# Fewer visits of TensorE to transposes, scores and values, and y's parts in the norm's tiles

## The chip, the core and the metric

The kernel runs on one core of one Trainium2 chip. The metric is the device time of one execution in microseconds (us). TensorE is the matmul engine (PE in the profile, PEld its weight loads), VectorE is DVE, ScalarE is ACT, GpSimd is POOL and SyncE is SP. Each engine works through its own queue of instructions in the order in which the program issues them, and waits on semaphores for the others.

## What is computed

The reference is one layer on 256 tokens of width 1024. Cut to what matters here:

```python
h = _rmsnorm(x, norm_w) * (1 + scale) + shift
(qa, ka, va, za, qm, km, vm, zm, om, ig, fg, ga, gm) = split(h @ w_in)
qa, ka = _rmsnorm(heads(qa, 8)), _rmsnorm(heads(ka, 8))
ya = (attention(qa, ka, va, rel_bias) * silu(za)) @ w_att_proj      # causal, 8 heads of 128
qm, km = split(silu(causal_conv(concat(qm, km))))
hm = mlstm(qm, km, vm, ig, fg)                                      # 4 heads of 256
ym = (rmsnorm(sigmoid(om) * hm) * silu(zm)) @ w_ml_proj
y = sigmoid(ga) * ya + sigmoid(gm) * ym
return x + gate * (y @ w_out)
```

All is float32. The large products are made of three fp32r matmuls: each operand is split into a high part and a low rest (names that end in h and l), and high x high, high x low and low x high are added up in PSUM.

## The kernel before

The first part, up to about 52 us, makes the norm (tiles hTh and hTl, h transposed, high and low part) and the first columns of h @ w_in. The rest, with which the change deals, is a list of 25 chunks of 512 output columns: the rest of ka, then two halves each of va, za, qm, km, att (the product with w_att_proj), zm, vm, om, ga, gm, ml (with w_ml_proj) and out (with w_out). A chunk has four steps, one for each pair of 128-row blocks of the weights, so that there are 100 steps: va is steps 4 to 11, za 12 to 19, qm 20 to 27, km 28 to 35, att 36 to 43, zm 44 to 51, vm 52 to 59, om 60 to 67, ga 68 to 75, gm 76 to 83, ml 84 to 91, out 92 to 99. A step is either 12 matmuls with 512 moving columns (kind "tok", lines L932 to L934, the activations are the stationary operand: va, zm, vm, om, out) or 24 matmuls with 256 moving columns (kind "ws", L939 to L942, the weights are the stationary operand: the others). For each step ScalarE casts the weights' high part (L424) and VectorE, for a few steps GpSimd, subtracts it (L428), four steps ahead of TensorE, into a ring of five buffers (wh, wl).

Between the matmuls of one step and the next, small work is put in by hand: at(step, function) calls the function just ahead of the step's matmuls, in the order in which the calls were registered, and between(step, function) calls it a little earlier, between the cast and the subtraction for the step four later. TensorE's share of this work are plain fp32 matmuls and transposes. One such stay of TensorE away from the weights' stream is called a visit here. The functions that matter:

- qk_T(which, half) transposes four heads of q or k: eight transposes (L468), four into each of two PSUM tiles named aux, and ScalarE copies each tile out (L470) to qT or kT.
- att_qk(h) (L577, L578): the scores of head h into an aux tile, which VectorE reads (L581, L583). att_exp(h): ScalarE's exponentials (L589, L590). att_norm(h): VectorE divides by the sums. att_PT(h): three transposes of the probabilities (L602 to L604).
- att_av(h0): probabilities times values for two heads (L615, L617). ml_scores(h): L716, L719. ml_T(kp): four transposes (L773) of mLSTM's result.
- gates_1, gates_2: small work on the gates. ScalarE's L512 in gates_2 waits for GpSimd's L505 in gates_1.
- ev_ml: makes y out of the last sums, with a cast to its high part and a subtraction for the low part (L705 to L708).

The aux tiles rotate over four PSUM banks in the order in which the program makes them: an aux tile can be written when the tile four before it has been read. mm tiles, the sums of a chunk, have two further places. SBUF is a set of named slots (s0 to s6, "bias"); a slot holds tiles that live one after the other, and FREE puts unused columns ahead of a slot, so that it sets where the tiles after it lie.

Of the kernel before, what the change touches and what calls it, by code (L numbers as in the profile page):

```python
# [10 lines left out]
F32R = mybir.dt.float32r  # L11
# [5 lines left out]
S = 256  # L17
KT = 8
# [46 lines left out]
def tile_hybrid(ctx: ExitStack, tc: tile.TileContext, x, c, params, params2, rel_t, w_row, ada_mod, ada_gate,  # L65
# [23 lines left out]
    hTh = consts.tile([128, KT, S], F32R, name="hTh")  # L89
    hTl = consts.tile([128, KT, S], F32R, name="hTl")  # L90
# [189 lines left out]
    for step in P1_STEPS:  # L280
        op, k = step[0], int(step[1])
# [42 lines left out]
    def done(name, half):  # L324
        return 4 * (C[name, half] + 1)
# [68 lines left out]
    SL = {}  # L394


    FREE = {'s2': 112, 's1': 80}

    def free(tag):
        if tag in FREE:  # L400
            hl.tile([128, FREE.pop(tag)], F32, name="free_" + tag, bufs=1)

    def slot(tag, shape, dt, name):
        free(tag)
        return hl.tile(shape, dt, name=name, tag=tag, bufs=1)
# [27 lines left out]
    def at(step, fn, *a):  # L433
        hooks.setdefault(step, []).append((fn, a))

    def between(step, fn, *a):
        hooks_between.setdefault(step, []).append((fn, a))

    T = {}
# [256 lines left out]

    def ev_ml(pt, half):
        if half == 0:
            for nm, tag, at0 in (("yh", "s2", 16), ("yl", "s6", 48)):
                t = slot(tag, [128, at0 + KT * S], F32R, nm)  # L700
                T[nm] = t[:, at0:].rearrange("p (k s) -> p k s", k=KT)
        for q in range(2):
            ks = slice(4 * half + 2 * q, 4 * half + 2 * q + 2)
            yf = hl.tile([128, 2, 256], F32, name="yf", tag="scr", bufs=2)
            nc.vector.tensor_tensor(yf, pt[:, 2 * q:2 * q + 2], T["gm"][:, ks], op=OP.mult)  # L705
            nc.vector.tensor_tensor(yf, yf, T["ga"][:, ks], op=OP.add)
            nc.scalar.copy(T["yh"][:, ks], yf)
            nc.vector.tensor_tensor(T["yl"][:, ks], yf, T["yh"][:, ks].bitcast(F32), op=OP.subtract)  # L708
# [97 lines left out]
    def ev_out(pt, c0, n, t):  # L806
# [5 lines left out]

    EV = dict(va=ev_va, za=ev_za, att=ev_att,
              zm=ev_zm, vm=ev_vm, om=ev_om, ga=ev_ga, gm=ev_gm, ml=ev_ml)

    at(0, q_scale)
# [7 lines left out]
    at(3, qk_norm, "q", 1)  # L824
    at(0, bias_read)
    at(4, gates_0)
    at(6, qk_T, "q", 0)
    at(7, qk_T, "k", 0)
    at(8, qk_T, "q", 1)
    at(7, qk_norm, "k", 1)  # L830
    at(10, qk_T, "k", 1)
    for h in range(AH):
        between(10 + h, att_norm, h)
        between(9 + h, att_qk, h)
        at(11 + h, att_PT, h)
        at(9 + h, att_exp, h)
    for step, fn in ((5, gates_1), (8, gates_2), (10, gates_3), (12, gates_copy), (13, gates_4), (15, gates_5),
                     (17, gates_6), (17, gates_T), (18, gates_7), (21, gates_D)):
        at(step, fn)
    for nm in ("qm", "km"):  # L840
        for hf in range(2):
            s = done(nm, hf)
# [2 lines left out]
                at(s + q + 1, conv_silu, hf, nm, q)  # L845
    for q in range(2):
        at(done("za", 0) + 1 + q, att_av, 2 * q)
        at(done("za", 1) + 1 + q, att_av, 4 + 2 * q)
    s = done("km", 0)
    at(s + 3, ml_scores, 0)  # L850
    at(s + 4, ml_scores, 1)
    s = done("km", 1)
    at(s + 3, ml_scores, 2)
    at(s + 4, ml_scores, 3)
    at(4 * C["att", 0] - 10, gate_init)
    gate_left = {}
    for q, nm in enumerate(GSEG):
        s = 4 * C[nm, 0] - 4
# [5 lines left out]
    for hp in range(2):  # L864
        s = done("om", hp)
        at(s + 1, ml_num, 2 * hp)
        at(s + 2, ml_num, 2 * hp + 1)
        at(s + 3, ml_y, hp)
        at(s + 7, ml_T, 2 * hp)
        at(s + 8, ml_T, 2 * hp + 1)  # L870

    A = HB - 1
# [21 lines left out]
    for g in range(NG):  # L894
# [30 lines left out]
        for kk in range(2):  # L925
            k = 2 * kp + kk
# [74 lines left out]
```

## Time and profile before

| | |
|---|---|
| median of 3 runs | 356.29 us (356.02 to 356.61) |
| the profiled execution | 356.5 us |
| its span (first to last instruction) | 354.7 us |
| granted TensorE clock, mean | 0.998 |
| busy: PE, PEld, DVE, ACT, POOL | 99%, 90%, 67%, 60%, 22% |
| read from HBM | 76.12 MB, 219 GB/s read and written |

In rows in order of time the columns are the start and the duration in us, the engine, the line, the operation, the tile written and the tiles read, the shape and how many instructions are merged into the row. A bracket at the end says how long the engine was idle before and what released it. A matmul's duration is longer than its share of the engine, as matmuls overlap; what counts is the distance from start to start. Chain rows give shares of the span by engine.

### The profile page before, as it was taken

What the parts mean: (1) busy time and instruction counts of PE and PEld (TensorE: products, weight loads), DVE (VectorE), ACT (ScalarE), POOL (GpSimd) and SP (SyncE); (2) the same over time, 40 slices, a digit from 0 to 9 for tenths busy, and PEclk for the clock granted to TensorE, in tenths of its full rate; (3) what the DMA queues carried; (4) which work ended last, traced back from release to release, by engine and by line L of the source; (5) the groups of instructions that cost most, each with busy time, mean ns of one, the idle gap of its engine ahead of it and who ended that gap; (6) DMA issues with size and microseconds to landing.
All of it is one profiled execution on the core that took longest, in us unless ns stands there. A gap on an engine that the chain in (4) does not pass through costs nothing.

```text
span 354.7 us, 5959 instructions
## 1 busy us (share of the span) xinstructions
PE 349.5 (99%) x2344; PEld 319.7 (90%) x2344; DVE 237.5 (67%) x362; ACT 212.3 (60%) x329; POOL 79.7 (22%) x88
## 2 busy tenths in 40 slices
PE   8999999999999999999999999999999999999995
PEld 5988889888999999999999888888899999999885
DVE  3998985898965527767875474764475775448773
ACT  3776797989886776765555444544646374544320
POOL 4940003775003234554340000000010420000000
PEclk9999999999999999999999999999999999999999
DMA  7999999994581264394673965749209219290011
GB/s 284 415 420 421 415 372 357 232 270 188 207 279 53 93 232 152 102 397 153 212 266 121 346 230 200 291 130 376 86 16 370 90 60 368 108 355 3 2 59 59
DMA packets 24573, 77.95 MB, mean 220 GB/s; under 512 B 2909, under 2 KB 5985, under 8 KB 24034
## 3 DMA queue, kind: packets, MB, share of 16 engines
q1 hardware_dynamic: 24240, 77.03, 61.1%
q10 hardware_dynamic: 306, 0.55, 0.5%
q8 instruction: 18, 0.29, 0.3%
q14 instruction: 9, 0.07, 0.1%
HBM read 76.12 MB, written 1.45 MB: 219 GB/s over the span
## 4 chain that ended last, share of the span: by engine, by line
PE 82%; DMA 8%; POOL 3%; DVE 2%; ACT 2%; issue 1%; SPq 0%; DVEq 0%; POOLq 0%; ACTq 0%
PE mm L942 15%; PE mm L939 14%; PE mm L941 14%; PE mm L932 8%; DMA raw<-in_w_row_dram 8%; PE mm L933 8%; PE mm L934 8%; PE pm L186 4%; POOL ms L454 2%; PE mm L953 1%; PE mm L951 1%; PE aux L615 1%; PE mm L952 1%; PE aux L716 1%; POOL ms L453 1%
## 5 line engine op out<-in xcount | busy, mean ns | idle before, releaser
L428 DVE TENSOR_TENSOR wl<-raw,wh 128x1024 fp32r<-128x1024 f32 (+1 forms) x92 | 113.1, 1241 | 70.3 <-ACT wh L424 70.3
L424 ACT CAST wh<-raw 128x1024 fp32r<-128x1024 f32 (+1 forms) x100 | 102.0, 1031 | 56.4 <-PE mm L934 28.7
L939 PE MATMUL mm<-hTh,wh 128*128 128x256 f32 x320 | 90.1, 282 | 0.0
L942 PE MATMUL mm<-hTh,wl 128*128 128x256 f32 x320 | 89.0, 278 | 0.0
L941 PE MATMUL mm<-hTl,wh 128*128 128x256 f32 x320 | 89.0, 278 | 0.0
L939 PEld LDWEIGHTS mm<-hTh,wh 128*128 128x128 f32 x320 | 60.5, 189 | 0.0
L941 PEld LDWEIGHTS mm<-hTl,wh 128*128 128x128 f32 x320 | 60.2, 188 | 0.0
L942 PEld LDWEIGHTS mm<-hTh,wl 128*128 128x128 f32 x320 | 60.1, 188 | 0.0
L932 PE MATMUL mm<-wh,hTh 128*128 128x512 f32 (+1 forms) x144 | 55.0, 382 | 0.0
L934 PE MATMUL mm<-wh,hTl 128*128 128x512 f32 (+1 forms) x144 | 54.4, 377 | 0.0
L933 PE MATMUL mm<-wl,hTh 128*128 128x512 f32 (+1 forms) x144 | 54.3, 377 | 0.0
L934 PEld LDWEIGHTS mm<-wh,hTl 128*128 128x128 f32 x144 | 27.0, 188 | 5.1
L932 PEld LDWEIGHTS mm<-wh,hTh 128*128 128x128 f32 x144 | 27.0, 188 | 4.7
L933 PEld LDWEIGHTS mm<-wl,hTh 128*128 128x128 f32 x144 | 27.1, 188 | 4.6
L428 POOL TENSOR_TENSOR wl<-raw,wh 128x1024 fp32r<-128x1024 f32 x8 | 19.5, 2460 | 18.0 <-ACT wh L424 18.0
L755 POOL TENSOR_SCALAR f<-f 128x4 f32<-128x4 f32 x2 | 0.4, 200 | 86.9 <-DVE f L754 86.9
L175 DVE TENSOR_TENSOR wrl<-raw,wrh 128x512 fp32r<-128x512 f32 (+1 forms) x24 | 18.2, 780 | 0.7 <-ACT wrh L170 0.3
L939 PE MATMUL mm<-yah,wh 128*128 128x256 f32 x64 | 18.0, 281 | 0.0
L941 PE MATMUL mm<-yal,wh 128*128 128x256 f32 x64 | 17.7, 277 | 0.0
L942 PE MATMUL mm<-yah,wl 128*128 128x256 f32 x64 | 17.7, 277 | 0.0
L939 PE MATMUL mm<-ymh,wh 128*128 128x256 f32 x64 | 17.7, 276 | 0.0
L941 PE MATMUL mm<-yml,wh 128*128 128x256 f32 x64 | 17.7, 276 | 0.0
(209 smaller groups left out, 650.1 us busy)
## 6 DMA issues: line engine op xcount, KB each, us to landing
raw<-in_w_in_dram SPq DMA_DIRECT2D x36, 1024.0 KB, 5.1
adat<-in_ada_mod_dram SPq DMA_DIRECT2D x16, 512.0 KB, 9.4
raw<-in_ada_gate_dram SPq DMA_DIRECT2D x4, 1024.0 KB, 5.6
raw<-in_w_att_proj_dram SPq DMA_DIRECT2D x4, 1024.0 KB, 7.8
raw<-in_w_ml_proj_dram SPq DMA_DIRECT2D x4, 1024.0 KB, 5.9
raw<-in_w_out_dram SPq DMA_DIRECT2D x4, 1024.0 KB, 6.3
raw<-in_w_row_dram SPq DMA_DIRECT2D x4, 896.0 KB, 12.1
raw<-in_w_row_dram SPq DMA_DIRECT2D x4, 640.0 KB
```

What stands on the lines that cost most here:

```text
L175: e.tensor_tensor(l[:, cs], wrow[k][:, cs], h[:, cs].bitcast(F32), op=OP.subtract)
L186: nc.tensor.matmul(pm[ch][:, t], a[:, k, t * 128:(t + 1) * 128], b[:, cs], start=k == 0 and i == 0 and (ch < 3 or t == 0), stop=k == KT - ...
L424: nc.scalar.copy(h, w)
L428: e.tensor_tensor(l, w, h.bitcast(F32), op=OP.subtract)
L453: nc.gpsimd.tensor_scalar(ms, ms, 1.0 / AD, EPS, op0=OP.mult, op1=OP.add)
L454: nc.gpsimd.tensor_tensor(ms, ms, mhalf[:, 0:8], op=OP.pow)
L932: nc.tensor.matmul(o, a, wh[:, kk], start=first, stop=False)
L933: nc.tensor.matmul(o, a, wl[:, kk], start=False, stop=False)
L934: nc.tensor.matmul(o, b, wh[:, kk], start=False, stop=last)
L939: nc.tensor.matmul(o, wh[:, kk, cs], sh_[:, k], start=first and i % 2 == 0, stop=False, skip_group_check=True)
L941: nc.tensor.matmul(o, wh[:, kk, cs], sl_[:, k], start=False, stop=False, skip_group_check=True)
L942: nc.tensor.matmul(o, wl[:, kk, cs], sh_[:, k], start=False, stop=last and i % 2 == 1, skip_group_check=True)
```

## The change

1. The q transposes of the first half move from step 6 to step 7, ahead of the k transposes there. Those of the second half move from step 8 to step 9, and the call is registered behind the loop over the heads, so that at step 9 it comes after att_qk and att_exp of head 0.
2. att_av of the last four heads: both calls at step 22, in place of 21 and 22. ml_scores of heads 0 and 1: both at step 36, in place of 35 and 36; of heads 2 and 3: both at step 40, in place of 39 and 40. ml_T of parts 0 and 1: both at step 72, in place of 71 and 72; of parts 2 and 3: both at step 76, in place of 75 and 76.
3. ev_ml writes y's high and low part into hTh and hTl, in place of tiles of their own in slots s2 and s6 (with offsets of 16 and 48 columns). FREE grows by 16 columns ahead of s1 and gets 48 ahead of s4: with this the tiles of all other slots stay at their addresses; only the small scratch tiles behind s2 move, by 64 bytes.

```diff
-    FREE = {'s2': 112, 's1': 80}
+    FREE = {'s2': 112, 's1': 96, 's4': 48}
...
-            for nm, tag, at0 in (("yh", "s2", 16), ("yl", "s6", 48)):
-                t = slot(tag, [128, at0 + KT * S], F32R, nm)
-                T[nm] = t[:, at0:].rearrange("p (k s) -> p k s", k=KT)
+            T["yh"], T["yl"] = hTh, hTl
...
-    at(6, qk_T, "q", 0)
+    at(7, qk_T, "q", 0)
     at(7, qk_T, "k", 0)
-    at(8, qk_T, "q", 1)
     at(7, qk_norm, "k", 1)
     at(10, qk_T, "k", 1)
     for h in range(AH):
         between(10 + h, att_norm, h)
         between(9 + h, att_qk, h)
         at(11 + h, att_PT, h)
         at(9 + h, att_exp, h)
+    at(9, qk_T, "q", 1)
...
-        at(done("za", 1) + 1 + q, att_av, 4 + 2 * q)
+        at(done("za", 1) + 2, att_av, 4 + 2 * q)
...
-    at(s + 3, ml_scores, 0)
+    at(s + 4, ml_scores, 0)
...
-    at(s + 3, ml_scores, 2)
+    at(s + 4, ml_scores, 2)
...
-        at(s + 7, ml_T, 2 * hp)
+        at(s + 8, ml_T, 2 * hp)
```

Below, numbers behind a tile's name tell its buffers apart, and a bracket names the engines waited for. Lines behind 699 have numbers lower by two in the changed kernel.

ScalarE's queue before, from the copy-out of va's first half (step 8) to the copy-outs of the k transposes (step 10):

```order
L629 COPY vat_827<-mm_720 128x2x512
L470 ACTIVATE qT_590<-aux_830,qns_77 128x512 [waits PE_49]
L470 ACTIVATE qT_590<-aux_836,qns_77 128x512 [waits PE_49]
L512 ACT_TABLE_LOAD
L512 ACTIVATE G_721<-G_721 4x256 [waits Pool_49]
L424 CAST wh_855<-raw_609 128x1024 [waits DMAHW2_49,DVE_49,PE_49]
L589 ACT_TABLE_LOAD
L589 ACTIVATE P_862,st_863<-P_862,st_863 128x256 [waits DVE_49]
L590 ACTIVATE P_862,st_863<-P_862,st_863 128x128 [waits DVE_49]
L424 CAST wh_881<-raw_653 128x1024 [waits DMAHW7_49,PE_49]
L470 ACTIVATE kT_619<-aux_895,prm2_68 128x512 [waits PE_49]
L470 ACTIVATE kT_619<-aux_901,prm2_68 128x512 [waits PE_49]
```

The same stretch of ScalarE's queue after the change:

```order
L629 COPY vat_828<-mm_720 128x2x512
L512 ACT_TABLE_LOAD
L512 ACTIVATE G_721<-G_721 4x256 [waits Pool_49]
L424 CAST wh_844<-raw_609 128x1024 [waits DMAHW2_49,DVE_49,PE_49]
L589 ACT_TABLE_LOAD
L589 ACTIVATE P_851,st_852<-P_851,st_852 128x256 [waits DVE_49]
L590 ACTIVATE P_851,st_852<-P_851,st_852 128x128 [waits DVE_49]
L470 ACTIVATE qT_590<-aux_858,qns_77 128x512 [waits PE_49]
L470 ACTIVATE qT_590<-aux_864,qns_77 128x512 [waits PE_49]
L424 CAST wh_882<-raw_653 128x1024 [waits DMAHW7_49,PE_49]
L470 ACTIVATE kT_619<-aux_896,prm2_68 128x512 [waits PE_49]
L470 ACTIVATE kT_619<-aux_902,prm2_68 128x512 [waits PE_49]
```

The two copy-outs of q have moved from ahead of L512 to behind head 0's exponentials.

TensorE's queue before, the visit of step 10 (scores of head 1, then the k transposes of the second half):

```order
L577 MATMUL aux_887<-kT_619,qT_590 128x256 [waits Activation_49]
L578 MATMUL aux_887<-kT_619,qT_590 128x128
L468 MATMUL aux_895<-ident_65,kt_618 128x128 [waits DVE_49,Activation_49]
L468 MATMUL aux_895<-ident_65,kt_618 128x128 x3
L468 MATMUL aux_901<-ident_65,kt_618 128x128 [waits Activation_49]
L468 MATMUL aux_901<-ident_65,kt_618 128x128 x3
```

The same visit after the change:

```order
L577 MATMUL aux_888<-kT_619,qT_590 128x256 [waits Activation_49]
L578 MATMUL aux_888<-kT_619,qT_590 128x128
L468 MATMUL aux_896<-ident_65,kt_618 128x128 [waits DVE_49]
L468 MATMUL aux_896<-ident_65,kt_618 128x128 x3
L468 MATMUL aux_902<-ident_65,kt_618 128x128 [waits Activation_49]
L468 MATMUL aux_902<-ident_65,kt_618 128x128 x3
```

The instructions are the same; what differs is which tile held each bank before. The program makes the aux tiles before in the order 830, 836 (q, second half), 859 (scores of head 0), 887, 895, 901, and after in the order 848 (scores of head 0), 858, 864 (q, second half), 888, 896, 902. So aux_895 and aux_901 follow 830 and 836, and aux_896 and aux_902 follow 848 and 858.

## Prediction

> **What bounds the kernel now.** I read the page first, then the list of what each engine waited for, then the engines' rows in order of time around the places that the change touches. Times are microseconds from the span's start; a step is one of the program's 100 groups of matmuls, as the text ahead explains.
>
> ```profile
> span 354.7 us, 5959 instructions
> PE 349.5 (99%) x2344; PEld 319.7 (90%) x2344; DVE 237.5 (67%) x362; ACT 212.3 (60%) x329; POOL 79.7 (22%) x88
> PE 82%; DMA 8%; POOL 3%; DVE 2%; ACT 2%; issue 1%; SPq 0%; DVEq 0%; POOLq 0%; ACTq 0%
> ```
>
> TensorE is busy for 99% of the span and holds 82% of the chain that ended last. The other shares of that chain lie early, before the weights stream freely. So a microsecond taken from TensorE's stream is a microsecond of the result, and a microsecond in which TensorE stands still while it streams is lost for good, unless a later wait of its own is shortened by it. The profiled execution took 356.5, 1.8 outside its span; the median of the runs is 356.29. I sum against 356.50 and take 0.21 off at the end.
>
> TensorE before, steps 10 and 11. The first two rows are att_qk of head 1, the third the k transposes of the second half, 82.69 starts step 11:
>
> ```profile
> 78.39 0.59 PE L577 MATMUL aux<-kT,qT 128*128 128x256 f32 x2
> 78.82 0.38 PE L578 MATMUL aux<-kT,qT 128*128 128x128 f32 x2
> 79.04 1.04 PE L468 MATMUL aux<-ident,kt 128*128 128x128 f32 x8
> 79.83 0.48 PE L932 MATMUL mm<-wh,hTh 128*128 128x512 f32 x1
> ...
> 82.69 0.59 PE L577 MATMUL aux<-kT,qT 128*128 128x256 f32 x2
> 83.12 0.38 PE L578 MATMUL aux<-kT,qT 128*128 128x128 f32 x2
> 83.61 0.33 PE L602 MATMUL aux<-ident,P 128*128 128x128 f32 x1
> 83.78 0.27 PE L603 MATMUL aux<-ident,P 128*128 128x128 f32 x1
> 83.89 0.27 PE L604 MATMUL aux<-ident,P 128*128 128x128 f32 x1
> ```
>
> One fp32 matmul of 128 columns takes 0.11 from start to start (83.78 to 83.89). At step 10 nothing waits: 79.04 follows 78.82 by two such. At step 11 the L602 at 83.61 comes 0.27 later than 83.12 + 0.22 allows: TensorE waits there for the first head's probabilities.
>
> ScalarE over the same time, with the GpSimd row it waits for and VectorE's last read of att_qk's bank for head 0:
>
> ```profile
> 74.79 1.29 ACT L470 ACTIVATE qT<-aux,qns 128x512 f32<-128x512 f32 x2
> 78.43 0.42 ACT L512 ACTIVATE G<-G 4x256 f32<-4x256 f32 x1 [1.05 <-POOL G L505]
> 78.87 1.05 ACT L424 CAST wh<-raw 128x1024 fp32r<-128x1024 f32 x1
> 79.94 1.28 ACT L589 ACT_TABLE_LOAD   x1
> 81.23 0.51 ACT L589 ACTIVATE P<-P,st 128x256 f32<-128x256 f32 x1
> 82.03 0.19 ACT L590 ACTIVATION_READ_ACCUMULATOR P<-P,st 128x1 f32 x1
> 82.13 1.03 ACT L424 CAST wh<-raw 128x1024 fp32r<-128x1024 f32 x1
> 76.75 1.65 POOL L505 TENSOR_SCALAR G<-G 4x256 f32<-4x256 f32 x1
> 79.49 0.08 DVE L583 DVE_READ_ACCUMULATOR2_ANT st<- 128x1 f32 x1
> ```
>
> ScalarE stands still for 1.05 until GpSimd's L505 ends at 78.40, then does L512, a cast, a table load and head 0's exponentials, which end at 82.22. Before, the copy-outs of the q transposes (L470, 74.79) stood ahead of that wait and were hidden by it.
>
> **The q transposes of the second half, steps 8 to 9.** They now stand behind head 0's exponentials on ScalarE, since the call is placed after att_exp. GpSimd's and VectorE's queues are unchanged here and nothing that feeds L505 moved, so the exponentials end at 82.22 as before. The first copy-out then takes the place of the cast at 82.13; half of 1.29 later, near 82.78, its PSUM bank is free. That is the bank that the last four k transposes of step 10 write, four aux tiles later. TensorE reaches them at 79.04 + 0.5 for the first four, which wait for VectorE's 79.57 in the other bank: so at 79.04 + 0.53 + 0.44 = 80.01. It stands still from there to about 82.83 (0.05 for the signal, as from VectorE's end at 67.63 to TensorE's 67.68 below). Before, these four began at 79.04 + 0.44 = 79.48. Loss: 82.83 - 79.48 = 3.35. The wait of 0.27 at step 11 is then covered: **+3.08**. Queued behind the wait are all matmuls from step 10 on. ScalarE's own queue from there is 1.2 later, which TensorE's 3.08 covers.
>
> **The q transposes of the first half, steps 6 to 7.**
>
> ```profile
> 66.41 1.22 DVE L459 TENSOR_TENSOR kt<-kt,ms 128x1024 f32<-128x1024 f32 x1
> 67.68 1.09 PE L468 MATMUL aux<-ident,kt 128*128 128x128 f32 x8
> ```
>
> The k transposes wait for VectorE's product, which ends at 67.63. The eight q transposes (8 x 0.11 = 0.87) now fill the time just ahead of 67.68, and the k transposes start when they did: 0.00. Whatever were gained here the wait of step 10 would swallow, since ScalarE sets its end.
>
> **A visit by itself.** Leaving the fp32r stream for four transposes and coming back:
>
> ```profile
> 269.54 0.60 PE L773 MATMUL aux<-ident,omt 128*128 128x128 f32 x4
> 269.89 0.37 PE L939 MATMUL mm<-hTh,wh 128*128 128x256 f32 x1
> 270.10 0.28 PE L941 MATMUL mm<-hTl,wh 128*128 128x256 f32 x1
> ```
>
> From 269.54 to 270.10 are 0.56; four transposes at 0.11 and one matmul at 0.113 make 0.553. A visit costs about 0.01 beyond its own work. Five fewer behind step 11: **-0.05**.
>
> **The pace after a visit.** The same 24 matmuls of 256 columns run at one of two paces, and a visit can switch it. Of the rows, pairs lie 23 matmuls apart (87.83, 90.54 and 162.98, 165.69), 71 apart (273.27, 281.64) and 144 apart (288.11, 304.43):
>
> ```profile
> 87.83 0.28 PE L941 MATMUL mm<-hTl,wh 128*128 128x256 f32 x1
> 90.54 0.38 PE L577 MATMUL aux<-kT,qT 128*128 128x256 f32 x1
> 161.56 1.02 PE L716 MATMUL aux<-qmT,kmT 128*128 128x256 f32 x4
> 162.98 0.28 PE L941 MATMUL mm<-hTl,wh 128*128 128x256 f32 x1
> 165.69 1.03 PE L716 MATMUL aux<-qmT,kmT 128*128 128x256 f32 x4
> 273.27 0.28 PE L941 MATMUL mm<-hTl,wh 128*128 128x256 f32 x1
> 281.64 0.38 PE L773 MATMUL aux<-ident,omt 128*128 128x128 f32 x2
> 288.11 0.28 PE L941 MATMUL mm<-hTl,wh 128*128 128x256 f32 x1
> 304.43 0.28 PE L941 MATMUL mm<-hTl,wh 128*128 128x256 f32 x1
> ```
>
> 2.71 / 23 = 0.118, twice, and 8.37 / 71 = 0.118 are slow; 16.32 / 144 = 0.113 is fast. A slow step costs 24 x 0.0046 = 0.11. What the trace of before cannot show is the pace behind a joint visit. I let each joint visit leave the pace that the second of its pair leaves now, as it ends with the same instructions at the same place. Then step 35 (162.98) and, in the same way, step 39 turn fast, 2 x -0.11; step 21 loses the visit that made it fast, +0.11; step 75 (the visit at 281.64 goes) stays slow, +0.11. Sum **0.00**. Bounds: all joint visits fast, -0.44 for steps 72 to 75; on the other side, a slow pace behind the joint visit of step 22, 36 or 40, 72, or 76 lasts 14, 4, 4 or 16 steps.
>
> **y's parts in the norm's tiles.** Casts and subtractions are the same in number and shape, and the tiles are free in time: their last readers are gm's matmuls (to step 83), and y is first written at step 88. What changes is the address that the stationary operand of w_out's matmuls is read from. 72 matmuls of 512 columns with y, and 72 of zm with hTh:
>
> ```profile
> 196.99 0.39 PE L932 MATMUL mm<-wh,hTh 128*128 128x512 f32 x1
> 213.31 0.39 PE L932 MATMUL mm<-wh,hTh 128*128 128x512 f32 x1
> 328.79 0.39 PE L932 MATMUL mm<-wh,yh 128*128 128x512 f32 x1
> 345.48 0.28 PE L951 MATMUL mm<-wh,yh 128*128 128x256 f32 x1
> ```
>
> 16.32 against 16.69: with y the stream is slow by 0.37. If the address does it, this goes, less some 0.03 for the entry: **-0.34**. If the entry from the 256-column stream does it, 0. I take -0.34, as zm too is entered from such a stream and runs fast.
>
> **Sum.** 356.50 + 3.08 + 0.00 - 0.05 + 0.00 - 0.34 = 359.19; against the median of 356.29 that is 358.98, so **359.0**.
>
> [...] The stall leaves TensorE with nothing but four transposes from 79.6 to 82.8. [...]
>
> **Rivals.** *The bank is free in time* (0.10). If the copy-out ran before 79.5, there would be no stall, and the rest gives 356.29 - 0.39 = 355.9, not slower than before; with all joint visits fast 355.5. It decides at ScalarE's L512: GpSimd's result would have to come some 3 earlier. Against it: the 1.05 of ScalarE's idle time ends on L505, whose inputs are not moved.
> *A joint visit leaves the slow pace on a long stretch* (0.25): behind step 22, 14 x 0.11 = 1.5, so 360.5; behind step 76, 16 x 0.11 = 1.8, so 360.8. For it: the two visits of one pair (269.54 and 272.72) leave different paces now.
> [...]
>
> **Numbers.** The forecast has 0.58. Its own range is 358.0 (all joint visits fast, and some of the slow steps from 87.83 on, 0.11 each, turned too) to 359.5 (no gain from y). For 8 in 10 I reach up to the long slow stretch and leave out the cooled array and most of the free bank: 357.5 to 360.9. 0.2%, 0.7, is about what a measurement of this kernel can tell from no change. Slower by more: 0.58 + 0.25 + 0.07, less 0.01 for what I overlooked, 0.89. The free bank and that 0.01 split into 0.06 within and 0.05 faster.
>
> **What would show it.** In the profile of the changed kernel: TensorE's L468 for the second half of k in two pieces, the second near 82.8, with ScalarE's L470 for q at 82.1; no wait of TensorE at step 11, which starts near 86.0 in place of 82.69; 24 matmuls in 2.72 in steps 35 and 39; w_out's 72 in 16.35. I am wrong if that L468 follows att_qk without a gap, and mis-sized if the gap is there but a long stretch changes its pace.

## The result and the profile after

The change makes the kernel slower: 360.88 us (median of 6 runs, 359.06 to 362.23) against 356.08 (355.99 to 356.61, 6 runs) of the kernel before, a ratio of 1.0125 [1.0096, 1.0154]. The forecast of 359.0 had the side and the place right, and was 1.9 short: 2.7 more than the 356.29 of three runs was forecast, 4.8 more than the 356.08 of six was measured. The six runs are not alike, and their mean granted clock sorts them: 359.06 at 1.000, 359.73 at 0.999, 360.83, 360.94 and 360.99 at 0.995, 362.23 at 0.991. The profiled one took 360.99. A stretch of 3.4 us at half the clock, as the trace below has one, is worth 1.7 / 359 = 0.005 of the mean: so by this estimate 0.995 stands for one such stretch and 0.991 for two.

The page of the changed kernel: the span, the engines' busy time, the granted clock in 40 slices, the chain that ended last by engine.

```profile
span 359.2 us, 5958 instructions
PE 350.6 (98%) x2344; PEld 321.1 (89%) x2344; DVE 236.7 (66%) x362; ACT 212.9 (59%) x329; POOL 77.9 (22%) x88
PEclk9999999998999999999999999999999999999999
PE 76%; DMA 8%; POOL 4%; DVE 4%; ACT 3%; issue 3%; SPq 0%; DVEq 0%; ACTq 0%; POOLq 0%
```

TensorE's share of the chain falls from 82% to 76%. That is not the wait alone: before 58 us the chain now runs over VectorE and ScalarE, where it ran over TensorE's matmuls before, though the work there is the same. Behind the wait, from 82.55 us on, it is TensorE's up to the last matmul. The one 8 in PEclk is the slice from 80.8 to 89.8 us, the stretch of steps 10 and 11, where TensorE's rows in order of time read:

```profile
78.22 0.59 PE L577 MATMUL aux<-kT,qT 128*128 128x256 f32 x2
78.65 0.38 PE L578 MATMUL aux<-kT,qT 128*128 128x128 f32 x2
79.32 0.65 PE L468 MATMUL aux<-ident,kt 128*128 128x128 f32 x4 [0.29 <-DVE st L583]
82.55 0.66 PE L468 MATMUL aux<-ident,kt 128*128 128x128 f32 x4 [2.57 <-ACT qT L470]
82.96 0.48 PE L930 MATMUL mm<-wh,hTh 128*128 128x512 f32 x1
...
84.09 0.63 PE L931 MATMUL mm<-wl,hTh 128*128 128x512 f32 x1
84.52 0.63 PE L932 MATMUL mm<-wh,hTl 128*128 128x512 f32 x1
...
87.39 0.59 PE L577 MATMUL aux<-kT,qT 128*128 128x256 f32 x2
87.82 0.38 PE L578 MATMUL aux<-kT,qT 128*128 128x128 f32 x2
88.04 0.27 PE L602 MATMUL aux<-ident,P 128*128 128x128 f32 x1
```

There are two losses in these rows. The k transposes are in two pieces, and the second waits 2.57 for the copy-out of q. From att_qk's start to the first matmul of the weights are now 82.96 - 78.22 = 4.74, before 79.83 - 78.39 = 1.44: 3.30 more. Then the 12 matmuls of step 10 last from 82.96 to 87.39, 4.43, where they took 2.86 before. One starts 0.43 behind the other (84.09 to 84.52) in place of 0.23 (the prediction's 16.69 / 72). At step 11, which starts at 87.39, nothing waits any more: 88.04 follows 87.82 by two times 0.11.

ScalarE's rows over the same time:

```profile
78.14 0.42 ACT L512 ACTIVATE G<-G 4x256 f32<-4x256 f32 x1 [2.23 <-POOL G L505]
78.58 1.04 ACT L424 CAST wh<-raw 128x1024 fp32r<-128x1024 f32 x1
79.64 1.28 ACT L589 ACT_TABLE_LOAD   x1
80.94 0.51 ACT L589 ACTIVATE P<-P,st 128x256 f32<-128x256 f32 x1
...
81.74 0.18 ACT L590 ACTIVATION_READ_ACCUMULATOR P<-P,st 128x1 f32 x1
81.83 1.24 ACT L470 ACTIVATE qT<-aux,qns 128x512 f32<-128x512 f32 x2
```

ScalarE stands still for 2.23 ahead of L512, where it stood still for 1.05 before: the copy-outs that used that time now come at 81.83, behind the exponentials. Half of 1.24 after 81.83 the first bank is free, and TensorE goes on at 82.55.

The windows of the changed kernel, 1 us each. The columns are the stretch, its length, then busy share and instructions of PE, PEld, DVE, ACT and POOL, then the granted clock, the DMA share and GB/s:

```profile
80.00:81.00 1.00, 0.00 (x0) 0.00 (x0) 1.00 (x1) 0.99 (x2) 0.92 (x2) 1.00 1.03 422
82.00:83.00 1.00, 0.45 (x5) 0.45 (x5) 0.96 (x6) 1.00 (x3) 0.01 (x1) 1.00 0.79 324
83.00:84.00 1.00, 1.00 (x6) 0.87 (x5) 0.26 (x4) 1.00 (x3) 0.00 (x0) 0.91 0.51 209
84.00:85.00 1.00, 1.00 (x4) 0.71 (x4) 0.96 (x1) 1.00 (x3) 0.00 (x0) 0.50 0.53 217
86.00:87.00 1.00, 1.00 (x3) 0.79 (x3) 0.72 (x3) 0.46 (x2) 0.37 (x1) 0.50 0.19 78
87.00:88.00 1.00, 1.00 (x6) 0.82 (x5) 0.00 (x0) 0.41 (x1) 0.92 (x2) 0.89 0.02 8
```

The clock is whole while TensorE stands still (1.00 from 80 to 83), halves at about 83.8 (0.91 is 0.18 us at half) when it has been at work again for 1.25, since 82.55, and is whole again from about 87.2 (0.89). That is one stretch of some 3.4 us. In it the busy share of PE is 1.00 at a clock of 0.50, with 0.43 from one matmul to the next in place of 0.23: the busy share alone doesn't show this loss.

Of the joint visits, two whose rows show the pace behind them (the first at step 36, the other at step 72; each pair of rows 23 matmuls apart):

```profile
171.53 0.28 PE L939 MATMUL mm<-yal,wh 128*128 128x256 f32 x1
174.13 0.28 PE L937 MATMUL mm<-yah,wh 128*128 128x256 f32 x1
277.53 0.28 PE L939 MATMUL mm<-hTl,wh 128*128 128x256 f32 x1
280.24 0.28 PE L937 MATMUL mm<-hTh,wh 128*128 128x256 f32 x1
```

2.60 / 23 = 0.113 is the fast pace, 2.71 / 23 = 0.118 the slow one. And w_out with y in the norm's tiles, the first matmul, the first of the last 24 with 512 columns, the first and the last of the 48 with 256 columns that end the kernel:

```profile
333.14 0.40 PE L930 MATMUL mm<-wh,hTh 128*128 128x512 f32 x1
344.05 0.39 PE L949 MATMUL mm<-wh,hTh 128*128 128x512 f32 x1
349.49 0.28 PE L949 MATMUL mm<-wh,hTh 128*128 128x256 f32 x1
355.12 0.28 PE L951 MATMUL mm<-wh,hTl 128*128 128x256 f32 x1
```

72 matmuls of 512 columns take 349.49 - 333.14 = 16.35, before 16.69. But the last 48 take 355.12 - 349.49 = 5.63. Before, the last of them started here, 5.33 after the 345.48 of the prediction's row:

```profile
350.81 0.28 PE L953 MATMUL mm<-wh,yl 128*128 128x256 f32 x1
```

### The profile page after: what moved, and what is told of

It is laid out like the page before. It is cut to its first block, busy times and chain, and to the rows that moved or that the text cites. A ratio compares the mean times of both kernels' runs of the same rounds, so it can differ in the third digit from the quotient of the medians.

```text
span 359.2 us, 5958 instructions
## 1 busy us (share of the span) xinstructions
PE 350.6 (98%) x2344; PEld 321.1 (89%) x2344; DVE 236.7 (66%) x362; ACT 212.9 (59%) x329; POOL 77.9 (22%) x88
## 4 chain that ended last, share of the span: by engine, by line
PE 76%; DMA 8%; POOL 4%; DVE 4%; ACT 3%; issue 3%; SPq 0%; DVEq 0%; ACTq 0%; POOLq 0%
PE mm L939 14%; PE mm L940 14%; PE mm L937 14%; DMA raw<-in_w_row_dram 8%; PE mm L931 8%; PE mm L930 8%; PE mm L932 8%; POOL ms L454 3%; DVE wrl L175 1%; POOL ms L453 1%; PE mm L951 1%; PE mm L949 1%; PE mm L950 1%; PE aux L615 1%; DVE ms L452 1%
## 5 line engine op out<-in xcount | busy, mean ns | idle before, releaser
L937 PE MATMUL mm<-hTh,wh 128*128 128x256 f32 x320 | 89.8, 281 | 0.0
L930 PE MATMUL mm<-wh,hTh 128*128 128x512 f32 (+1 forms) x160 | 61.7, 386 | 0.0
L931 PE MATMUL mm<-wl,hTh 128*128 128x512 f32 (+1 forms) x160 | 61.4, 384 | 0.0
L932 PE MATMUL mm<-wh,hTl 128*128 128x512 f32 (+1 forms) x160 | 61.1, 382 | 0.0
L932 PEld LDWEIGHTS mm<-wh,hTl 128*128 128x128 f32 x160 | 30.5, 190 | 5.8
L931 PEld LDWEIGHTS mm<-wl,hTh 128*128 128x128 f32 x160 | 30.4, 190 | 5.8 <-DVE wl L428 0.4
L930 PEld LDWEIGHTS mm<-wh,hTh 128*128 128x128 f32 x160 | 30.3, 190 | 5.5
L940 PE MATMUL mm<-ymh,wl 128*128 128x256 f32 x64 | 17.7, 276 | 0.0
```

The costliest lines, as they stand in the source:

```text
L930: nc.tensor.matmul(o, a, wh[:, kk], start=first, stop=False)
L931: nc.tensor.matmul(o, a, wl[:, kk], start=False, stop=False)
L932: nc.tensor.matmul(o, b, wh[:, kk], start=False, stop=last)
L937: nc.tensor.matmul(o, wh[:, kk, cs], sh_[:, k], start=first and i % 2 == 0, stop=False, skip_group_check=True)
L940: nc.tensor.matmul(o, wl[:, kk, cs], sh_[:, k], start=False, stop=last and i % 2 == 1, skip_group_check=True)
```

## The experiments

The theory: the q transposes of the second half, put behind head 0's exponentials, make TensorE wait at step 10; that costs some 3 us. What is beyond 3 us is the halved clock, which follows from TensorE standing still; the joint visits and y are worth little. The first rival: a joint visit leaves the slow pace on a long stretch. The second: the place of the wait is right, but what costs the rest is not the clock. Times from the trace "from step 4 on" run from va's first matmul to the last matmul; they repeat closely where the start of step 4 itself moves between runs by up to 1.3 (57.63 to 58.90). Before they are 292.39, after 296.85, so +4.46.

**Which part makes it slower.** a_q1_back is the changed kernel with that one call put back:

```diff
     at(7, qk_T, "k", 0)
+    at(8, qk_T, "q", 1)
...
-    at(9, qk_T, "q", 1)
```

> The changed kernel with one call put back: the q transposes of the second half at step 8. Theory (ScalarE copies these transposes out behind head 0's exponentials, so the k transposes of step 10 wait for their bank): no wait of TensorE at step 10, and the time is the median before, 356.1, less 0.05 for the visits, less 0.22 for steps 35 and 39, plus 0.22 for steps 21 and 75, less 0.06 for y (0.34 less in 72 matmuls, 0.28 more in the last 48, by the changed kernel's trace): 356.0, and the runs lie within 1 us of each other. Rival (the joint visits or y's new place cost the time): it stays above 358.

Measured: 356.45 (356.11 to 357.20) against 356.21, ratio 1.0007 [0.9998, 1.0016]. In its trace nothing waits at step 10, and from step 4 on it takes 292.26.

b_q1_only is the kernel before with that one call moved, and nothing else:

```diff
-    at(8, qk_T, "q", 1)
...
+    at(9, qk_T, "q", 1)
```

> The kernel before with one call changed: the q transposes of the second half at step 9, behind att_exp. Theory: TensorE waits some 2.6 to 2.8 for the bank at step 10, 356.1 + 3.1 = 359.2 where the clock stays whole and 1.7 more for each window at half clock behind the wait, so 359 to 361 with runs that differ by 1.7. Rival (the joint visits or y's place): 357 or less.

Measured: 360.79 (360.49 to 361.12, 4 runs), ratio 1.0127 [1.0113, 1.0140]. Its waits are those of the changed kernel, 0.3 and 2.6, and the clock is 0.995 in each of the four runs. In its trace the clock halves at 82.8 (0.89 is 0.22 us at half), as TensorE goes on at 82.73, and is whole again from 86.2:

```profile
82.00:83.00 1.00, 0.27 (x2) 0.28 (x3) 0.83 (x4) 1.00 (x4) 0.18 (x1) 0.89 0.83 340
83.00:84.00 1.00, 1.00 (x5) 0.97 (x5) 0.43 (x4) 1.00 (x2) 0.00 (x0) 0.50 0.52 213
86.00:87.00 1.00, 1.00 (x5) 0.79 (x5) 0.71 (x3) 0.63 (x3) 0.20 (x1) 0.91 0.13 53
```

So this one call is the whole loss, in both directions, and the other parts together come to nothing that can be told: the long slow stretch falls.

**Standing still, or the clock.** c_fill is the changed kernel with ten needless fp32 matmuls of 128 columns (20 instructions; their result is overwritten) just ahead of the k transposes of step 10, where TensorE would stand still:

```diff
+            for _ in range(10 if (which, h0) == ("k", 4) else 0):
+                nc.tensor.matmul(pa[:, 0, 0:128], tok[:, half, 0, 0:128], ident, start=True, stop=True)
```

> The changed kernel with ten more fp32 matmuls of 128 columns (20 instructions, 2.2 us) ahead of the first four k transposes of step 10, into the same tile, which the transposes then overwrite; the result is the same. Theory (the half clock behind the wait comes from TensorE's idle time, and costs 1.7 of the 4.8): the copy-out still sets the end of the wait, the clock stays whole, and the time falls to 359.1 although TensorE does more, in every run, with less than 1 between runs. Rival (the half clock has nothing to do with the idle time): 360.9 with the same spread. Rival (the wait is shorter than the row says): 362 or more, as the added work comes on top.

Measured: 359.42 (358.90 to 359.67), ratio 1.0090 [1.0075, 1.0106], at a clock of 0.998 to 1.000. TensorE's rows:

```profile
78.86 2.50 PE L467 MATMUL aux<-ident,kt 128*128 128x128 f32 x20 [0.30 <-DVE st L585]
81.20 0.60 PE L470 MATMUL aux<-ident,kt 128*128 128x128 f32 x4
82.09 0.66 PE L470 MATMUL aux<-ident,kt 128*128 128x128 f32 x4 [0.29 <-ACT qT L472]
```

The delay is still there, now filled with needless work: from step 4 to the start of step 12 it takes 32.26, before 29.21, so +3.05; the changed kernel takes 33.77. With this work added, the kernel is faster than without it by 360.88 - 359.42 = 1.5. That is the clock's part, and 3.05 is the delay's.

g_fill_T does the same with 20 transposes in place of the matmuls:

```diff
+            for _ in range(20 if (which, h0) == ("k", 4) else 0):
+                nc.tensor.transpose(pa[:, 0, 0:128], tok[:, half, 0, 0:128], ident)
```

> As the run that filled the wait of step 10 with fp32 matmuls, but with twenty transposes (2.2 us again) in their place. Theory 1 (any work of the array keeps the clock whole): 359.4 as with the matmuls, no half clock in step 10. [...]

Measured: 359.60 (358.85 to 360.15), ratio 1.0092 [1.0072, 1.0111], at 0.997 to 0.999; from step 4 on 295.38, c_fill 295.34. In its trace the mean clock is 0.999, in c_fill's 1.000, where the one halved stretch of the changed kernel's gives 0.995: transposes of fp32 kept the clock whole here as matmuls did. (A mean of 0.997 or 0.998 needs no stall: in the trace of the kernel before, at 0.998, the clock halves only at 353.1, two microseconds behind the last matmul.)

**What sets the end of the wait.** Two obstacles stand ahead of the copy-out on ScalarE: L512, which waits for GpSimd, and the table load with head 0's exponentials. f_q1_ahead takes the second away, by registering the same call ahead of att_exp. TensorE's order is that of the changed kernel:

```diff
+    at(9, qk_T, "q", 1)
     for h in range(AH):
...
-    at(9, qk_T, "q", 1)
```

> The changed kernel with the q transposes of the second half at step 9 as it has them (TensorE's order is the same), but registered ahead of att_exp, so that ScalarE copies them out ahead of head 0's exponentials. Theory (the place in ScalarE's queue sets the wait, not TensorE's visits): the first copy-out ends near 80.6, TensorE waits 0.3 and 0.6 at step 10, the clock stays whole; step 11 starts near 83.95 in place of 82.69 and its wait of 0.27 is gone, so 356.2 + 1.0 = 357.2. Rival (the joint visit of step 9 itself costs the 3 us): 359 to 361 as the changed kernel.

Measured: 357.66 (357.31 to 358.26), ratio 1.0040 [1.0027, 1.0053]. ScalarE's and TensorE's rows:

```profile
77.79 0.42 ACT L512 ACTIVATE G<-G 4x256 f32<-4x256 f32 x1 [2.23 <-POOL G L505]
78.23 1.04 ACT L424 CAST wh<-raw 128x1024 fp32r<-128x1024 f32 x1
79.18 1.26 ACT L470 ACTIVATE qT<-aux,qns 128x512 f32<-128x512 f32 x2
```

```profile
79.91 1.24 PE L468 MATMUL aux<-ident,kt 128*128 128x128 f32 x8 [1.23 <-ACT qT L470]
```

TensorE waits 1.23 in one piece, where 0.3 and 0.6 in two were expected, and the clock stays whole (0.999 to 1.000 in the six runs). k_gates_late takes the first obstacle away instead, by moving gates_2 (L512) from step 8 to step 9, behind the copy-outs:

```diff
-    for step, fn in ((5, gates_1), (8, gates_2), (10, gates_3), (12, gates_copy), (13, gates_4), (15, gates_5),
+    for step, fn in ((5, gates_1), (9, gates_2), (10, gates_3), (12, gates_copy), (13, gates_4), (15, gates_5),
```

> The changed kernel with gates_2 (ScalarE's L512 and its table load) at step 9, behind head 0's exponentials and the copy-outs of q, in place of step 8 ahead of them. TensorE's order is the same. Theory (the wait of step 10 is as long as ScalarE takes to reach the copy-out, and 2.6 of that is L512's wait for GpSimd with the table loads around it): the exponentials start when VectorE has read head 0's scores, near 79.6, the first copy-out ends near 81.1, TensorE waits about 1.4 in place of 2.57 for it, the clock stays whole: 357.7. Rival (TensorE waits for something else that comes at a fixed time near 82.6): 359 to 361 as the changed kernel.

Measured: 357.61 (357.13 to 359.09, 6 runs), ratio 1.0041 [1.0025, 1.0057].

```profile
79.08 0.66 PE L468 MATMUL aux<-ident,kt 128*128 128x128 f32 x4 [0.29 <-DVE st L583]
80.46 0.66 PE L468 MATMUL aux<-ident,kt 128*128 128x128 f32 x4 [0.72 <-ACT qT L470]
```

The wait for the copy-out falls from 2.57 to 0.72 (1.4 was expected), by 1.85, and the time from c_fill's whole-clock 359.42 to 357.61, by 1.8. Either obstacle alone is enough to make TensorE wait; only the place before both (a_q1_back) is free.

d_k1_late leaves q's call at step 9 and takes away the demand for the bank: the k transposes of the second half move from step 10 to step 12.

```diff
-    at(10, qk_T, "k", 1)
+    at(12, qk_T, "k", 1)
```

> The changed kernel with the k transposes of the second half at step 12 in place of 10, where the bank that they follow is that of head 0's transposed probabilities; the q transposes stay behind att_exp. Theory: no wait for a copy-out at step 10, step 11 waits some 0.3 for head 0's probabilities as before, 356.0 with all seven visits saved. Rival (the copy-outs behind the exponentials delay ScalarE by 1.2, which TensorE then waits for in steps 11 to 13): 357 to 358.

Measured: 356.68 (356.27 to 357.61), ratio 1.0015 [1.0006, 1.0024], where 356.0 was expected. The stall is gone, but TensorE waits at step 11:

```profile
83.02 0.30 PE L602 MATMUL aux<-ident,P 128*128 128x128 f32 x1 [0.41 <-DVE P L597]
```

The k transposes had filled time at step 10 in which head 0's probabilities became ready. Without them TensorE reaches step 11 earlier, waits 0.41 there, and does their 0.87 at step 12 all the same: counted from step 4, step 12 starts 0.40 later than before.

**The visits and their pace.** e_pairs is the kernel before with the joint ml_scores and with ml_T put together at the earlier step of each pair (71 and 75) in place of the later:

```diff
-    at(s + 3, ml_scores, 0)
+    at(s + 4, ml_scores, 0)
...
-    at(s + 3, ml_scores, 2)
+    at(s + 4, ml_scores, 2)
...
-        at(s + 8, ml_T, 2 * hp + 1)
+        at(s + 7, ml_T, 2 * hp + 1)
```

> The kernel before with three pairs put together and nothing else: ml_scores at steps 36 and 40 as in the change, and ml_T at steps 71 and 75, where the change has 72 and 76. Theory (a joint visit leaves the pace that a visit with the same instructions at the same place left): steps 35, 39 and 72 to 74 take 2.72 in place of 2.83, 5 x 0.11 less, and four visits' 0.01 less: 355.6. Rival (eight transposes leave the slow pace wherever they stand): steps 72 to 75 stay slow, 356.0.

Measured: 356.28 (355.68 to 356.99), ratio 1.0001 [0.9990, 1.0011], where 355.6 was expected. The joint visit at step 71 leaves the slow pace (2.83 for the 24 matmuls of step 72, and of 73, and of 74), the one at 75 the fast one (2.72 for step 76). It is again the pace that the second visit of each pair leaves in the kernel before, though at an earlier step. I had tied the rule to the place; in these pairs it goes with the visit. Why one visit leaves one pace and the next another, no run here shows.

h_scores_y is the kernel before with the two parts of the change that gain by the trace: joint ml_scores, as above, and y in the norm's tiles.

> The kernel before with the two parts of the change that the step times of the earlier runs speak for, and no other: ml_scores put together (0.10 at step 36 and 0.12 at step 40) and y's parts in the norm's tiles (0.07). Expected 356.2 less 0.29, 355.9; from the first matmul of va to the last matmul 292.10 in place of 292.39. Rival (a joint visit's pace is not settled by what stands in it): another pace behind steps 36 or 40, 0.4 more for each.

Measured: 355.92 (355.41 to 356.38, 11 runs) against 356.23, ratio 0.9992 [0.9983, 1.0001]; from step 4 on 292.12, 0.27 less than before, 0.23 of it by the scores (to step 44). It is the fastest of all these kernels, by less than can be told from no change.

**y's place.** y_only is the kernel before with y in the norm's tiles alone (the first two pieces of the change's diff).

> The kernel before with y's parts in the norm's tiles alone, and the filling that keeps the other addresses. By the changed kernel's trace the 72 matmuls of 512 columns gain 0.34 and the last 48 of 256 columns lose 0.28 to 0.30: 356.2 - 0.05, not to be told from before. Rival (the pace at the end was set by the joint visits, not by the addresses): the end is as before, 5.57 for 24 matmuls and 5.33 for the last 48.

Measured: 356.24 (355.57 to 356.83), ratio 0.9996 [0.9985, 1.0007]; from step 4 on 292.32, so -0.07. Its 24 matmuls of 512 columns take 5.44 (before 5.57), its last 48 of 256 columns 5.63 (before 5.33). y_at_0 keeps y in tiles of its own and changes nothing but the offset at which they begin:

```diff
-    FREE = {'s2': 112, 's1': 80}
+    FREE = {'s2': 112, 's1': 96, 's4': 48}
...
-            for nm, tag, at0 in (("yh", "s2", 16), ("yl", "s6", 48)):
+            for nm, tag, at0 in (("yh", "s2", 0), ("yl", "s6", 0)):
```

> The kernel before with y's two tiles in their own slots, 64 and 192 bytes further ahead (the offsets of 16 and 48 columns taken away), the other tiles where they were. If the address of the stationary operand sets the pace of w_out's matmuls, the 24 of 512 columns (5.57 before, 5.44 in the norm's tiles) or the last 48 of 256 (5.33 before, 5.63 in the norm's tiles) change; if it is the tile or the dependencies between its readers and writers, both stay at 5.57 and 5.33.

Measured: one run, 356.38; 5.44 and 5.63, the same as in the norm's tiles. So it is the address of y that sets both, not the sharing of the tiles. l_mix has the joint scores and mixes the offsets, 0 for the high part and 48 for the low part:

```diff
-    FREE = {'s2': 112, 's1': 80}
+    FREE = {'s2': 112, 's1': 96}
...
-            for nm, tag, at0 in (("yh", "s2", 16), ("yl", "s6", 48)):
+            for nm, tag, at0 in (("yh", "s2", 0), ("yl", "s6", 48)):
...
-    at(s + 3, ml_scores, 0)
+    at(s + 4, ml_scores, 0)
...
-    at(s + 3, ml_scores, 2)
+    at(s + 4, ml_scores, 2)
```

> The kernel before with ml_scores in joint visits (steps 36 and 40) and y's high part at offset 0, its low part at offset 48 as before. Two thirds of w_out's matmuls read the high part. If the high part's address alone sets w_out's pace, 24 matmuls of 512 columns take 5.44 (before 5.57) and the last 48 of 256 columns 5.63 (before 5.33), as with both parts at offset 0, and the time is that with y in the norm's tiles and joint scores, 355.9 in the call before. If the low part's address sets it, they take 5.57 and 5.33, and the time is that of the joint scores alone, 356.0. If both count, each pace lies between, by which of the 24 and of the 48 are fast; 5.44 with 5.33 would be the best of both: 355.65.

Measured: 356.16 (355.68 to 356.84) against 356.10, ratio 1.0002 [0.9992, 1.0011]; 5.55 and 5.53: the first is near the worse end, the second two thirds of the way to it. Its last matmuls, in which L951 and L952 read the high part and L953 the low:

```profile
345.64 0.28 PE L951 MATMUL mm<-wh,yh 128*128 128x256 f32 x1
345.76 0.28 PE L952 MATMUL mm<-wl,yh 128*128 128x256 f32 x1
345.88 0.28 PE L953 MATMUL mm<-wh,yl 128*128 128x256 f32 x1
345.99 0.28 PE L951 MATMUL mm<-wh,yh 128*128 128x256 f32 x1
```

A matmul that reads the high part at offset 0 takes 0.12, one that reads the low part at offset 48 takes 0.11: in this stream of 256 columns each goes by its own operand's address, and two thirds of the 0.30 are lost. In the stream of 512 columns that doesn't hold: with two thirds of the matmuls fast the 24 would take 5.48, and they take 5.55. Why, no run here shows. The best of both, 5.44 with 5.33, was not found.

## Why the prediction was right, and where it was not

**The stall of the second half of q: right.** Predicted were 3.35 less the 0.27 of step 11, so +3.08. Measured are 3.30 in the rows, and c_fill's +3.05 up to step 12, with the rest of the stall's way confirmed: copy-outs at 81.83 (82.1 predicted, in an execution that ran 0.3 earlier there), second piece at 82.55 (82.8), no wait at step 11. The free bank, the rival on the faster side, falls.

**The first half of q: right.** From step 4's first matmul to att_qk of step 10 the trace has 19.95, before 19.96: 0.00, as predicted.

**Visits and pace: right.** Predicted were -0.05 and 0.00. From step 20 to 23 the joint att_av costs 0.10, the joint ml_scores give 0.11 and 0.12 back (from step 23 to 36 and from 36 to 44), and from step 68 to 80 the joint ml_T cost 0.07: -0.06 in all. Each of the five joint visits left the pace that the second of its pair left before. The long slow stretch, to which I gave 0.25, falls with it.

**y in the norm's tiles: mis-sized.** The -0.34 for the 72 matmuls came as predicted. What I left out are the last 48 of 256 columns: they read the same y, from the same address, and lose 0.30 by it. The term is -0.04 in place of -0.34. I had a row of them in hand (345.48), and used it only as the end of the 72.

**The array's clock: the step that failed.** I gave a cooled array, by which the forecast means the clock halved behind the stall, 0.07, and left it out of the sum of the time. No run shows this 0.07: it was my estimate. What the runs showed in its place: in four of the six the mean clock is lower (0.991 to 0.995), and in the trace the halved stretch turns step 10's 2.86 into 4.43: +1.57, not 2.86 once more. Two things make the price smaller. The first matmuls of step 10 ran at the whole clock, and only 3.4 us from 83.8 on at half of it. And a matmul of 512 columns took 0.43 there in place of 0.23, a little less than twice. So step 11 starts at 87.39, where 86.0 was forecast. The sum by the trace: 3.30 - 0.27 + 1.57 - 0.06 - 0.04 = 4.50, against 4.46 measured from step 4 on. Without the halved clock, 356.29 + 3.03 - 0.10 = 359.2, and the two runs at whole clock have 359.06 and 359.73: so the forecast's number is that of the case that came up in two runs of six. That the measured 360.88 still lies within the stated 357.5 to 360.9 is luck: the upper end was drawn for a long slow stretch, which did not come, and the cooled array was meant to lie outside.

How long TensorE must stand still for the clock to halve was not shown: no run varied that time for its own sake. What was measured: behind a wait of 2.57 the clock was at half for 3.4 us in the traces of the changed kernel (83.8 to 87.2) and of b_q1_only (82.8 to 86.2). Behind one of 1.23 (f_q1_ahead, a mean of 0.999 in its trace), behind 0.29 and 0.72 (k_gates_late, 0.998) and behind 0.30 and 0.29 (c_fill, 1.000) there was no such stretch. Nor does the wait of 2.57 seem to bring it every time: of the ten runs of the changed kernel and of b_q1_only, eight have a mean of 0.995 or less and two of 0.999 or more. That the same kernel takes 359.1 in one run and 360.9 in another fits the estimate of 1.7 us for one such stretch. Why it came in one and not in the other, no run here shows: no trace of a changed kernel's run at whole clock was kept. Why the run of 362.2 has, by its mean clock of 0.991, two halved stretches stays open.

## What to carry to other kernels

When work is moved behind something on one engine, follow its buffer: the transposes moved by one step cost TensorE nothing, but their copy-out landed behind another engine's wait and a table load, and a bank that rotates four tiles later was not free. A stall of TensorE can have a second price in the clock behind it, here 1.5 us for one of 2.57 (in eight of ten runs) and nothing for one of 1.23, which shows as busy time; filling the stall with needless matmuls or transposes saved that part here (359.42 and 359.60 in place of 360.88). When an operand's address is changed, price every shape of matmul that reads it, as one may gain what another loses.

## What was not expected of the hardware

- The halved clock begins behind the idle time, and how far behind differs: with the same wait of 2.57, 1.25 us after TensorE went back to work in the changed kernel's trace (82.55 to 83.8), and at once in b_q1_only's (82.73 to 82.8). Both last 3.4 us.
- The clock halved behind a wait of 2.57 in the traces of the changed kernel and of b_q1_only (a mean of 0.995 in both), and did not behind one of 1.23 in f_q1_ahead's (0.999).
- The offset of the stationary operand sets the pace in opposite directions by shape: y at offset 0 takes 0.227 for 512 columns (16.35 / 72) and 0.120 for 256 (5.63 / 47), y at offsets 16 and 48 takes 0.232 (16.69 / 72) and 0.113 (5.33 / 47).
- Twenty fp32 transposes in a stall kept the clock whole in all four of their runs (0.997 to 0.999), as twenty matmul instructions did in four of theirs (0.998 to 1.000).
